# Twelve projection weights split during the first feed-forward stage, and the down weights of the passes loaded in pairs

## The chip, the cores and the metric

The kernel runs on one core of a Trainium2 chip. The metric is the device time of one execution in microseconds; the kernel before took 1989.62 us (median of three runs, 1989.21 to 1990.04). In what follows PE is the matmul engine, PEld its weight load, DVE the vector engine, ACT the scalar engine, POOL the GpSimd engine and SP the engine whose queue issues every DMA of this kernel.

## The reference, cut to what matters

One decoder layer on 1024 tokens with 16 meta tokens ahead of them, width 1024, all in float32:

```python
h = h + 0.5 * swiglu(rmsnorm(h, norm_ffn1), w_ffn1_gate, w_ffn1_up, w_ffn1_down)   # width 2816
u = rmsnorm(h, norm_mix)
qa, ka, va, qi, ki, wi, qs, ksw, vsw, ga, gb = split(u @ w_in)
# rope on qa, ka, qi, ki, qs, ksw
# sparse branch: scores from relu(qi . ki) * wi, the 256 largest keys, softmax attention with qa, ka, va
# window branch: 128 wide window with sinks, attention with qs, ksw, vsw
merged = sigmoid(ga) * (o_sparse @ w_branch_sparse) + sigmoid(gb) * (o_swa @ w_branch_swa)
h = h + merged @ w_out
h = h + 0.5 * swiglu(rmsnorm(h, norm_ffn2), w_ffn2_gate, w_ffn2_up, w_ffn2_down)
out = rmsnorm(h[:, BLOCK:], norm_final)
```

## The kernel before, in words

**Halves.** A float32 matrix is multiplied as two float16 halves, high and low. A weight tile of 128 rows arrives by DMA in a float32 buffer `wst` (two buffers). ACT writes its scaled high half into a float16 tile `wsp` (four buffers), and DVE writes the low half, which is the scaled weight less the high half (`split_w`, lines 428 to 431). PE then makes three products for each pair: high by high, high by low, low by high (`mm3`). A `wsp` buffer is free again when the last product that reads it is done.

**Stages.** The program is the first feed-forward network, the mixer (projections, rope, scores, the two attentions, the merge, the output projection) and the second feed-forward network. The tokens stand in two halves x = 0 and x = 1, of 528 and 512 columns.

**The feed-forward main part** multiplies 2 by 2 block matrices by seven products of quarter blocks (p1, p3 or p6, p7, p5, c11, p74, p53) and not eight, so each weight pair needs sums of its blocks first. One such round is a *joint* (lines 743 to 749); there are 32 of them, jobs 0 to 31, over gate, up and down weights. In joint i, `prepare(i + 1)` gives the steps that make job i + 1's weights: four sums or differences on DVE (tiles `sa`, `sb`), four high halves on ACT and four low halves on DVE (`wsp` for job halves x1 and x2, tiles x3 and x4 for the rest). The steps are put in a list `todo`, from which `pump` issues a share after each product; what is left is issued by `drain` at the joint's end. `fetch(i + 2)` issues the DMAs. The instructions issued this way have line 189 in the profile.

**The written order and the planner.** In the two stretches where `nc.on` is true, instructions are only recorded; `Plan.run` (lines 225 to 338) then orders them by a list schedule, taking on each engine the ready instruction of the lowest rank. The rank is the place in the program plus `nc.shift`. Instructions of a planned stretch have line 334. The planned stretches are: the beginning of the first network up to and with joint 0; everything from the end of the first network's main part to the end of the mixer; the beginning of the second network up to and with its joint 0; and the end. Joint 0 needs, besides `u` (the normalized input), the block sums `tb` of that input, which are made in the same stretch.

**The passes.** The last four of 22 blocks of the down projection, in each network, aren't done by joints but by a plain loop over x and over eight output blocks d: `load_w` loads a 128x512 weight, splits it, and PE multiplies (`pdn`), DVE adds to `h`.

**Projections in the mixer.** `k_half` and `q_groups` (lines 1187 to 1198) load two 128x1024 columns blocks of `w_in` each time (`load_w(win[...], 1024)`), for twenty loads in all: blocks 0 to 7 once for x = 0 and once for x = 1, blocks 8 to 11 once for both. They are used by `rope_split`, whose products are named `rp` in the profile.

```python
def load_w(src, n, st=None):
    ...
    sp = wsp_tile()
    nc.shift = -300
    split_w(sp, st, n)
    nc.shift = 0
    return sp
```

Of the kernel before, what the change touches and what calls it, by code (L numbers as in the profile page):

```python
# [11 lines left out]
F16 = mybir.dt.float16  # L12
F32 = mybir.dt.float32
I32 = mybir.dt.int32
U16 = mybir.dt.uint16
AF = mybir.ActivationFunctionType
ALU = mybir.AluOpType

P = 128
# [6 lines left out]
NF = DFF // P  # L26
# [10 lines left out]
WS = 256.0  # L37
# [316 lines left out]
def layer_kernel(ctx: ExitStack, tc: tile.TileContext, xT, gains, wgu1, wd1, win, wvi, wbs, wbw, wout,  # L354
# [78 lines left out]
    def wsp_tile():  # L433
        return new(big, [P, 2, 1024], F16, tag="wsp", name="wsp", bufs=4)

    def load_w(src, n, st=None):
        if st is None:
            st = load_raw(src, n)
# [5 lines that stand above are left out]
# [86 lines left out]
    def ffn(u, rb, hs, gi, wgu, wd, other_half, passes, saved, before_passes):  # L530
# [140 lines left out]
            split_w(x4, r2[:, hi], 512)  # L671
            return parts_of(x1, x2, x3, x4, 512)

        weights, fetched = {}, {}

        def fetch(i):
            if i < len(jobs):
                n = 2 * jobs[i][3]
                fetched[i] = [load_raw(src, n) for src in jobs[i][1:3]]

        def prepare(i):
            if i >= len(jobs):
                return []
            n = jobs[i][3]
            lo, hi, both = slice(0, n), slice(n, 2 * n), 2 * n
            r1, r2 = fetched.pop(i)
            x1, x2 = wsp_tile(), wsp_tile()
            sa, sb = sum_tiles()
            x3, x4 = late_tiles()
            weights[i] = parts_of(x1, x2, x3, x4, n)  # L690
            one, two = n / 750, n / 420
            v = nc.vector
            return [
                (0, lambda: high(x1, r1, both)),
                (one, lambda: v.tensor_add(sb[:, lo], r2[:, lo], r2[:, hi])),
                (0, lambda: high(x4, r2[:, hi], n)),
                (one, lambda: v.tensor_sub(sa[:, lo], sb[:, lo], r1[:, lo])),
                (one, lambda: v.tensor_sub(sa[:, hi], r1[:, lo], r2[:, lo])),
                (0, lambda: high(x2, sa, both)),
                (one, lambda: v.tensor_sub(sb[:, hi], r1[:, hi], sa[:, lo])),  # L700
                (two, lambda: low(x1, r1, both)),
                (one, lambda: low(x4, r2[:, hi], n)),
                (0, lambda: fetch(i + 1)),
                (0, lambda: high(x3, sb, both)),
                (two, lambda: low(x2, sa, both)),
                (two, lambda: low(x3, sb, both)),
            ]
# [32 lines left out]
        DOWN = ("p1", "p7", "p5", "p6", "c11", "p74", "p53")  # L740
        turn = [0]

        def joint(blocks, order):
            i = turn[0]
            turn[0] += 1
            own = prepare(i + 1)
            todo.extend(own[:7] + tail[:4] + own[7:10] + tail[4:] + own[10:])
            tail.clear()
            return fast(weights.pop(i), blocks, order)

# [304 lines left out]
        for x, subs, done in passes:  # L1055
# [1 line left out]
            full = c1 - c0 == hs[x][0].shape[1]  # L1057
            acc = new_acc()
            for d in range(KD):
                nd = (f1 - f0) * P  # L1060
                w = load_w(wd[d // 2][:, 2 * f0 * P + d % 2 * nd:2 * f0 * P + (d % 2 + 1) * nd], nd)
                if ph["mix"]:
                    for a, b in subs:
                        ps = mmps("pdn")[:, :b - a]
# [120 lines left out]
    wn = mcst([P, NB, 4], F32, "wn")  # L1185

    def k_half(x):
        w1, w2 = load_w(win[0], 1024), load_w(win[1], 1024)
        stack_k(rope_split(w1, w2, x, SUB_ALL[x]), kt[x], HW[x])

    def q_groups(xs, first, n):
        res = [[] for _ in xs]
        for g in range(n):
            w1 = load_w(win[first + 2 * g], 1024)
            w2 = load_w(win[first + 2 * g + 1], 1024)
            for lst, x in zip(res, xs):
                lst.append(q_half(w1, w2, x))
        return res
# [520 lines left out]
```

## Time and profile before

| what | us |
|---|---|
| median of three runs | 1989.62 |
| the profiled execution | 1987.38 |
| its span, first to last instruction | 1985.3 |
| PE busy in the span | 1918.0 |
| DVE busy | 1610.0 |
| ACT busy | 903.9 |
| POOL busy | 342.5 |

[...] The first network's main part runs from some 92 to 614 us, its passes to some 655, the mixer to 1340, the second network's main part to 1924. A busy PE is not always a PE at its peak: ends of matmuls are modelled and overlap the next one, so a short gap between two of them doesn't show as idle time. The page's chain of waits is 72% PE, 17% DVE, 6% ACT, 3% issue and 1% DMA.

### The profile page before, as it was taken

How to read it: one execution, taken by the hardware profiler on the slowest of the kernel's cores; microseconds unless marked ns; L12 is line 12 of the kernel's file. 1: busy time of each engine (PE TensorE's matmuls, PEld its weight loads, DVE VectorE, ACT ScalarE, POOL GpSimd, SP SyncE). 2: the span in 40 equal slices, each digit the busy share in tenths (PEclk: the TensorE clock that was granted, in tenths of full speed). 3: DMA queues.
4: the chain of work that ended last, by engine and by line, in shares of the span. 5: the costliest groups of instructions: out<-in, count | busy, mean ns of one | idle time of the engine just before them, and what ended most of it. 6: DMA issues, size and time to landing. Idle time of an engine off the chain costs nothing.

```text
span 1985.3 us, 32868 instructions
## 1 busy us (share of the span) xinstructions
PE 1918.0 (97%) x13080; PEld 1196.8 (60%) x13080; DVE 1610.0 (81%) x2809; ACT 903.9 (46%) x1621; POOL 342.5 (17%) x282
## 2 busy tenths in 40 slices
PE   6999999999998999899999999999899999999997
PEld 5688888888887656555545656444344444444443
DVE  7988788778775899999998967657987888788757
ACT  6533233233332546579876555435433333243232
POOL 0113311312210222221000000003312212312200
PEclk9999999999999999999999999999999999999998
DMA  5011211111222544221111231331112112111214
GB/s 173 22 60 49 65 64 49 59 65 38 70 75 87 185 150 132 69 91 44 45 37 49 92 112 38 128 122 39 47 53 66 53 58 58 54 64 50 78 33 138
DMA packets 60026, 146.96 MB, mean 74 GB/s; under 512 B 7392, under 2 KB 15584, under 8 KB 59872
## 3 DMA queue, kind: packets, MB, share of 16 engines
q1 hardware_dynamic: 59872, 144.87, 23.1%
q8 instruction: 102, 1.67, 0.4%
q14 instruction: 52, 0.43, 0.1%
HBM read 130.01 MB, written 14.76 MB: 73 GB/s over the span
## 4 chain that ended last, share of the span: by engine, by line
PE 72%; DVE 17%; ACT 6%; issue 3%; DMA 1%; SPq 0%; POOL 0%; DVEq 0%; ACTq 0%; POOLq 0%
PE pa L189 15%; PE pc L189 15%; PE pd L189 15%; PE pb L189 7%; PE p_gate L334 4%; PE p_out L334 4%; PE pdn L334 3%; DVE sc L334 3%; PE p_br L334 2%; DVE wsp L334 2%; ACT jk L334 2%; ACT psw L334 1%; DVE m L334 1%; PE rp L334 1%; DVE tb L334 1%
## 5 line engine op out<-in xcount | busy, mean ns | idle before, releaser
L189 PEld LDWEIGHTS <-wsp 128*128 128x128 f16 x4032 | 395.5, 98 | 205.7 <-DVE wsp L334 8.5
L334 PEld LDWEIGHTS <-wsp 128*128 128x128 f16 x3216 | 311.2, 99 | 295.9 <-issue 14.9
L189 PEld LDWEIGHTS <-x 128*128 128x128 f16 x3024 | 295.9, 98 | 145.1 <-issue 1.5
L189 PE MATMUL pa<-u,wsp 128*128 128x264 f16 (+1 forms) x1368 | 216.8, 313 | 7.8 <-DVE wsp L334 7.8
L334 PE MATMUL p_gate<-u,wsp 128*128 128x512 f16 x768 | 186.4, 379 | 0.0
L189 POOL TENSOR_TENSOR h<-h,base 128x512 f32<-128x512 f32 (+1 forms) x72 | 116.3, 1615 | 291.2 <-DVE base L189 210.5
L334 DVE SCALAR_TENSOR_TENSOR wsp<-wst,wsp 128x1024 f16<-128x1024 f32 (+2 forms) x131 | 133.1, 1019 | 38.7 <-ACT wsp L334 38.2
L334 ACT ACTIVATE wsp<-wst 128x1024 f16<-128x1024 f32 (+2 forms) x131 | 112.2, 861 | 92.3 <-PE p_out L334 28.5
L334 PE MATMUL rp<-u,wsp 128*128 128x512 f16 (+2 forms) x624 | 139.5, 365 | 3.9 <-DVE rt L334 3.5
L189 PE MATMUL pb<-tb,wsp 128*128 128x264 f16 (+1 forms) x684 | 106.8, 310 | 0.0
L189 PE MATMUL pc<-tb,x 128*128 128x264 f16 (+1 forms) x684 | 106.7, 310 | 0.1
L334 ACT ACTIVATE jk<-sc,s5nb 128x784 f16<-128x784 f32 (+2 forms) x93 | 98.0, 1054 | 16.1 <-DVE s5nb L334 14.7
L189 ACT ACTIVATE wsp<-wst 128x1024 f16<-128x1024 f32 (+1 forms) x60 | 57.9, 965 | 103.9 <-DMA wst<-in_wgu_dram 58.6
L189 PE MATMUL pd<-u,x 128*128 128x256 f16 (+1 forms) x684 | 105.2, 308 | 0.0
L189 PE MATMUL pc<-tb,wsp 128*128 128x256 f16 (+1 forms) x684 | 105.2, 308 | 0.0
L189 PE MATMUL pd<-tb,x 128*128 128x256 f16 (+1 forms) x684 | 105.2, 308 | 0.0
L189 PE MATMUL pa<-hid,wsp 128*128 128x264 f16 (+1 forms) x648 | 103.1, 310 | 0.0
L189 PE MATMUL pd<-hid,x 128*128 128x256 f16 (+1 forms) x648 | 101.6, 308 | 0.0
L189 ACT ACTIVATE wsp<-sa 128x1024 f16<-128x1024 f32 (+1 forms) x60 | 58.1, 968 | 95.3 <-DVE sa L189 95.3
L189 ACT ACTIVATE hid<-g 128x512 f16<-128x512 f32 (+1 forms) x54 | 33.2, 625 | 149.2 <-DVE g L189 149.2
L189 ACT ACTIVATE base<-pa 128x528 f32<-128x528 f32 (+1 forms) x62 | 37.1, 599 | 132.2 <-PE pa L189 132.2
L189 DVE TENSOR_TENSOR c<-pc,base 128x512 f32<-128x512 f32 x76 | 52.6, 692 | 55.1 <-PE pc L189 54.8
(238 smaller groups left out, 3478.0 us busy)
## 6 DMA issues: line engine op xcount, KB each, us to landing
wst<-in_wgu_dram SPq DMA_DIRECT2D x88, 512.0 KB, 4.0
wst<-in_win_dram SPq DMA_DIRECT2D x44, 512.0 KB, 3.5
wst<-in_wd_dram SPq DMA_DIRECT2D x48, 384.0 KB, 3.5
wst<-in_wd_dram SPq DMA_DIRECT2D x32, 256.0 KB, 2.9
wst<-in_wout_dram SPq DMA_DIRECT2D x16, 512.0 KB, 3.6
qscr<-ry SPq DMA_DIRECT2D x20, 256.0 KB, 2.2
q<-qscr SPq DMA_DIRECT2D x20, 256.0 KB, 3.0
wst<-in_wbs_dram SPq DMA_DIRECT2D x16, 256.0 KB, 3.3
```

The costliest lines, as they stand in the source:

```text
L189: return getattr(engine.real, op)(*[give(a) for a in args], **{k: give(v) for k, v in kw.items()})
L334: getattr(engine.real, op)(*[give(a) for a in args], **{k: give(v) for k, v in kw.items()})
```

## The change

Three edits are made.

1. *Ready weights.* In the first network's joints 1 to 25, one more group of steps, a *chore*, stands at the end of `todo`. A chore splits half a 128x1024 block of `w_in` (512 columns) into its float16 halves and stores them in device memory (`wready`); it also fetches the next half block. Twenty-four chores make the first twelve blocks. In the mixer, `load_ready` then loads the finished halves from device memory straight into a `wsp` tile, where `load_w` loaded float32 and split it. The buffers of the chores (`raw`, `pre`) come from the two buffers of tag `acc`.
2. *Pairs.* The passes load the down weights of two output blocks as one 128x1024 tile; two of the eight pairs of each network are fetched and split in joint 31, that is before the passes.
3. *Rank.* In `joint`, the weight steps of the next job are ranked by 300 places earlier (`ranked`). That has an effect only where the planner is on, so in joint 0 of each network.

```diff
+    ready = {}
+
+    def load_ready(m):
+        sp = wsp_tile()
+        nc.sync.dma_start(sp, ready[m])
+        return sp
+
+    def chores():
+        def fetch(c):
+            raw = new(big, [P, 528], F32, tag="acc", name="raw", bufs=2)
+            return raw, (0, lambda: nc.sync.dma_start(raw[:, :512], win[c // 2][:, c % 2 * 512:c % 2 * 512 + 512]))
+
+        def split(c, raw):
+            sp = new(big, [P, 2, 528], F16, tag="acc", name="pre", bufs=2)
+            if c % 2 == 0:
+                ready[c // 2] = new(dram, [P, 2, 1024], F16, name=f"wready{c // 2}")
+            dst = ready[c // 2][:, :, c % 2 * 512:c % 2 * 512 + 512]
+            return [(0, lambda: nc.scalar.activation(sp[:, 0, :512], raw[:, :512], AF.Copy, scale=WS)),
+                    (0.7, lambda: nc.vector.scalar_tensor_tensor(sp[:, 1, :512], raw[:, :512], WS, sp[:, 0, :512],
+                                                                 op0=ALU.mult, op1=ALU.subtract)),
+                    (0, lambda: nc.sync.dma_start(dst, sp[:, :, :512]))]
...
         def fetch(i):
-            if i < len(jobs):
+            if i == len(jobs):
+                fetched[i] = [load_raw(pair_src(d), 2 * ND) for d in range(2)]
+            elif i < len(jobs):
...
         def prepare(i):
-            if i >= len(jobs):
-                return []
+            if i == len(jobs):
+                ready_w.extend(wsp_tile() for _ in range(2))
+                return [(0, lambda op=op, x=x, r=r: op(x, r, 2 * ND)) for x, r in zip(ready_w, fetched.pop(i))
+                        for op in (high, low)]
...
+        def ranked(step):
+            def go():
+                was, nc.shift = nc.shift, -300
+                step()
+                nc.shift = was
+            return go
+
         def joint(blocks, order):
             i = turn[0]
             turn[0] += 1
-            own = prepare(i + 1)
+            own = [(c, ranked(step)) for c, step in prepare(i + 1)]
             todo.extend(own[:7] + tail[:4] + own[7:10] + tail[4:] + own[10:])
+            if gi == 0 and not nc.on and i % 1 == 0:
+                todo.extend(next(chore, []))
...
             for d in range(KD):
-                nd = (f1 - f0) * P
-                w = load_w(wd[d // 2][:, 2 * f0 * P + d % 2 * nd:2 * f0 * P + (d % 2 + 1) * nd], nd)
+                if d % 2 == 0:
+                    pair = ready_w.pop(0) if ready_w else load_w(pair_src(d // 2), 2 * ND)
+                w = pair[:, :, d % 2 * ND:(d % 2 + 1) * ND]
...
     def k_half(x):
-        w1, w2 = load_w(win[0], 1024), load_w(win[1], 1024)
+        w1, w2 = load_ready(0), load_ready(1)
...
-            w1 = load_w(win[first + 2 * g], 1024)
-            w2 = load_w(win[first + 2 * g + 1], 1024)
+            w1, w2 = load_ready(first + 2 * g), load_ready(first + 2 * g + 1)
```

The planner's order changes at several places; three of them matter later. On DVE, in the first network's joint 0 (planned), `wsp`, `sa`, `sb` and `x` are job 1's weight steps, `tb` and `tu` the block sums of the input and `hid` the hidden activations of the first blocks, which are needed only later. Before, the last rows of this stretch were:

```order
L334 TENSOR_TENSOR hid<-silu,hid 128x512
L334 SCALAR_TENSOR_TENSOR wsp<-wst,wsp 128x1024
L334 SCALAR_TENSOR_TENSOR x_592<-wst,x_592 128x512
L334 TENSOR_TENSOR hid<-silu,hid 128x528 x2
L334 SCALAR_TENSOR_TENSOR wsp<-sa,wsp 128x1024
L334 SCALAR_TENSOR_TENSOR x_992<-sb,x_992 128x1024
L189 TENSOR_TENSOR sb<-wst 128x512
```

Now the same steps stand between the second and the third group of `tb`, and the stretch ends with `hid` (`silu` here belongs to the first pair of blocks, `x_817` is job 1's x3):

```order
L334 SCALAR_TENSOR_TENSOR wsp<-wst,wsp 128x1024
L334 TENSOR_TENSOR sa<-sb,wst 128x512
L334 SCALAR_TENSOR_TENSOR silu<-pw,silu 128x512
L334 TENSOR_TENSOR sa<-wst 128x512
L334 TENSOR_TENSOR sb<-wst,sa 128x512
L334 SCALAR_TENSOR_TENSOR silu<-pw,silu 128x512
L334 SCALAR_TENSOR_TENSOR wsp<-sa,wsp 128x1024
L334 SCALAR_TENSOR_TENSOR x_817<-sb,x_817 128x1024
L334 TENSOR_TENSOR tu<-tu 128x512
```

So job 1's low halves moved from behind the last `tb` to a place ahead of two of the four `tb` groups. In the second network's joint 0 the move is of the same kind.

On SP's queue, at the beginning of the mixer, `wst<-in_win` were the float32 loads of projection weights, `hspill` stores of the residual, `kscr` and `k` the key's way through device memory. Before:

```order
L334 DMA wst<-in_win_dram 128x1024
L334 DMA hspill<-h 128x512 x2
L334 DMA wst<-in_win_dram 128x1024
L334 DMA hspill<-h 128x512
L334 DMA wst<-in_win_dram 128x1024
L334 DMA wst<-in_wvi_dram 128x980
L334 DMA wst<-in_wvi_dram 128x588
L334 DMA wst<-in_win_dram 128x1024
L334 DMA kscr<-ry 128x1056
```

Now (the numbers in `wready_...` tell the blocks apart):

```order
L334 DMA wsp<-wready_1684 128x2048
L334 DMA hspill<-h 128x512 x2
L334 DMA wsp<-wready_2087 128x2048
L334 DMA hspill<-h 128x512 x2
L334 DMA wsp<-wready_2426 128x2048
L334 DMA hspill<-h 128x512
L334 DMA wst<-in_wvi_dram 128x980
L334 DMA kscr<-ry 128x1056
```

The loads stand at about the same places of the queue, but they now write a `wsp` tile, and so wait for one to be free, where before they waited for a `wst` buffer.

## Rows read from the trace of the kernel before

**Rows 1.** Stretches: us, PE, PEld, DVE, ACT, POOL busy, clock, DMA, GB/s

```profile
...
92.00:614.00 522.00, 522.00 (x4694) 459.50 (x4692) 402.84 (x509) 172.52 (x251) 110.22 (x68) 1.00 0.19 59
614.00:655.00 41.00, 34.98 (x256) 25.51 (x254) 27.17 (x59) 16.50 (x31) 0.95 (x1) 0.96 0.48 150
655.00:905.00 250.00, 234.58 (x1766) 142.36 (x1765) 237.47 (x577) 153.23 (x367) 67.88 (x56) 0.99 0.38 122
905.00:1075.00 170.00, 168.81 (x1166) 89.76 (x1164) 159.41 (x475) 145.47 (x317) 7.62 (x37) 1.00 0.12 38
1075.00:1340.00 265.00, 264.03 (x1846) 144.60 (x1843) 192.32 (x373) 128.06 (x211) 6.04 (x24) 1.00 0.30 95
1340.00:1420.00 80.00, 70.38 (x313) 31.66 (x313) 68.66 (x85) 39.41 (x59) 33.72 (x20) 0.96 0.12 40
...
```

**Rows 2.** Chain of waits: start, us, what

```profile
1241.55 5.18 PE p_gate L334 x24
```

**Rows 3.** Timeline, joint 0 and job 1 of the first network

```profile
77.41 1.92 DVE L334 TENSOR_TENSOR tb<-tu,tb 128x512 f16<-128x512 f32 x3
...
86.60 0.61 PE L189 MATMUL pa<-u,wsp 128*128 128x264 f16 x4
...
90.96 3.83 PE L189 MATMUL pa<-u,wsp 128*128 128x264 f16 x20 [3.75 <-DVE wsp L334]
```

**Rows 4.** Timeline, joint 0 and job 1 of the second network

```profile
1387.37 2.29 DVE L334 SCALAR_TENSOR_TENSOR wsp<-sa,wsp 128x1024 f16<-128x1024 f32 x1
...
1406.42 0.67 DVE L334 TENSOR_TENSOR tb<-tu,tb 128x512 f16<-128x512 f32 x1
...
1409.68 0.59 PE L189 MATMUL pa<-u,wsp 128*128 128x512 f16 x2
...
1414.29 3.96 PE L189 MATMUL pa<-u,wsp 128*128 128x512 f16 x10 [4.01 <-DVE wsp L334]
...
1415.96 1.21 DVE L334 SCALAR_TENSOR_TENSOR wsp<-sa,wsp 128x1024 f16<-128x1024 f32 x1
```

**Rows 5.** Waits of PE, whole span: us in total, times, longest

```profile
...
PE pa L189 <- DVE wsp L334: 7.8, 2, 4.0
...
PE pdn L334 <- DVE wsp L334: 3.3, 1, 3.3
...
PE pdn L334 <- ACT wsp L334: 1.7, 1, 1.7
...
```

**Rows 6.** Timeline, first passes

```profile
616.56 1.30 DVE L189 TENSOR_TENSOR hid<-c,hid 128x528 f16<-128x528 f32 x2
...
619.27 6.79 PE L334 MATMUL pdn<-hid,wsp 128*128 128x272 f16 x44 [3.32 <-DVE wsp L334]
...
627.78 19.49 PE L334 MATMUL pdn<-hid,wsp 128*128 128x272 f16 x157 [1.71 <-ACT wsp L334]
```

**Rows 7.** Groups on DVE, then ACT, 614 to 905 us: busy, mean ns

```profile
L334 DVE SCALAR_TENSOR_TENSOR wsp<-wst,wsp 128x1024 f16<-128x1024 f32 x22 | 30.1, 1367 | 4.4 <-ACT wsp L334 4.4
...
L334 DVE SCALAR_TENSOR_TENSOR wsp<-wst,wsp 128x512 f16<-128x512 f32 x18 | 12.4, 699 | 1.5 <-ACT wsp L334 1.5
...
L334 ACT ACTIVATE wsp<-wst 128x1024 f16<-128x1024 f32 x22 | 23.0, 1049 | 14.4 <-PE rp L334 7.5 <-DMA wst<-in_win_dram 6.1 <-PE pv_t L334 0.7
```

**Rows 8.** Chain of waits, 655 to 905 us, shares by line

```profile
by line: DVE sc L334 11.8%; ACT psw L334 10.9%; PE rp L334 10.1%; issue 8.8%; DVE wsp L334 6.7%; DVE psw L334 5.7%; DVE rt L334 4.0%; DMA wst<-in_win_dram 3.8%; PE pv_t L334 3.7%; ACT wsp L334 3.7%; DVE pts L334 2.9%; DVE m L334 2.8%; ACT j
```

**Rows 9.** Stretch 655 to 905 us, tile wsp alone: PE, PEld, DVE, ACT busy

```profile
655.00:905.00 250.00, 182.15 (x937) 68.91 (x720) 37.69 (x31) 29.05 (x31) 0.99 0.38 122
```

**Rows 10.** DMA issues: KB each, us from issue to landing

```profile
wst<-in_win_dram SPq DMA_DIRECT2D x44, 512.0 KB, 3.5
```

**Rows 11.** Waits, 655 to 905 us: total, times, longest

```profile
ACT wsp L334 <- PE rp L334: 15.7, 7, 3.9
```

**Rows 12.** Group of 512-wide low halves in the joints: busy, mean ns

```profile
L189 DVE SCALAR_TENSOR_TENSOR x<-wst,x 128x512 f16<-128x512 f32 x36 | 24.5, 681 | 0.0
```

**Rows 13.** Timeline, end of a joint in the first network

```profile
110.79 0.69 DVE L189 TENSOR_TENSOR base<-pd,base 128x512 f32<-128x512 f32 x1 [1.17 <-PE pd L189]
```

More of the change, by code (lines that the diff above doesn't have):

```diff
@@ L434, in wsp_tile @@
         return new(big, [P, 2, 1024], F16, tag="wsp", name="wsp", bufs=4)
+    ready = {}
[16 more added lines that the diff above has]
+                    (0, lambda: nc.sync.dma_start(dst, sp[:, :, :512]))]
+        raw, step = fetch(0)
+        yield [step]
+        for c in range(24):
+            done = split(c, raw)
+            if c < 23:
+                raw, step = fetch(c + 1)
+                done.append(step)
+            yield done
+    chore = chores()
     def load_w(src, n, st=None):
@@ L672, in wide_weights, with pair_src @@
             return parts_of(x1, x2, x3, x4, 512)
-        weights, fetched = {}, {}
+        weights, fetched, ready_w = {}, {}, []
+        F0 = F_GROUPS[-1][0]
+        ND = (NF - F0) * P
+        def pair_src(j):
+            return wd[j][:, 2 * F0 * P:2 * F0 * P + 2 * ND]
         def fetch(i):
-            if i < len(jobs):
+            if i == len(jobs):
+                fetched[i] = [load_raw(pair_src(d), 2 * ND) for d in range(2)]
+            elif i < len(jobs):
                 n = 2 * jobs[i][3]
```

## The prediction

> **What bounds the kernel now.** I read the table by stretches first, then PE's waits, then the chain of waits in the one stretch where PE is not full, and last the timelines at the four places where the change moves something. In the first network's main part PE is busy for all of 522.00 us while DVE works 402.84 and ACT 172.52: PE bounds it, and DVE has 119 us to spare [rows 1]. In the passes PE is busy 34.98 of 41 us. In the mixer from 655 to 905 us PE is busy 234.58 of 250 and DVE 237.47 of 250, 95%: DVE is the fuller of the two. From 905 to 1340 PE is again above 99%, and DVE falls to 73% in the last 265 us. At the second network's start both have holes (70.38 and 68.66 of 80). So time can come back only where PE has holes: before 92 us, 614 to 905, 1340 to 1420 and in the tail. The idle time that the rows show from 614 to 905 is 6.0 + 15.4 = 21.4 us, and there is more that they hide: 24 matmuls of 512 columns take 5.18 us, so 216 ns each [rows 2], and every gap below a matmul's modelled end counts as busy.
>
> **The first joint of the first network (rank).** Before, PE came to job 1 at 86.60 us, did 4 matmuls and stood 3.75 us for a low half (`wsp`); the other 20 began at 90.96 [rows 3]. Taking 112 ns for one of the 4, PE started as if at 90.5. Now job 1's steps stand ahead of the last `tb` groups. From 77.41 us, 1.92 us for three, the last `tb` began at about 78.65 before [rows 3]. By the order, DVE now has ahead of it, in addition: three 1024-wide low halves (1.21 us each in [rows 4], some 1.15 from start to start), one 512-wide, four sums, one `hid` and two `c` (0.6 each), which is 8.25 us. The last `tb` then begins at 86.9 and the one before it ends at 86.4; PE still has 4 matmuls of p6 and the 24 of p74 to do, 0.45 + 2.7 us, and reaches job 1 at 89.6 with its weights ready. Gain 90.5 - 89.6 = 0.9 us. Bounds: -1 (another us of `tb`) and 3.8 (the whole stall).
>
> **The same in the second network.** PE reached job 1 at 1409.68, did 2, stood 4.01 us and went on at 1414.29, as if started at 1413.86 [rows 4]. The last `tb` began at 1406.42. Newly ahead of it: three 1024-wide low halves, one 512-wide and three sums, 5.8 us; gone from ahead: two `silu` and two `hid`, 2.4. So it begins 3.4 us later, at 1409.8, and the one before it ends near 1408.4; then 2 matmuls of p6 and 12 of p74 at 216 ns, 3.0 us: job 1 at 1411.2 or so. Gain 2.7 us. POOL is the risk here: next to its work the same low half took 2.29 us where it took 1.21 later [rows 4], and two such moved into that stretch leave 0.6. Bounds 0 and 4. [...]
>
> **The passes (pairs).** PE stood 3.32 us until 619.27 for the first low half and 1.71 us until 627.78 for a high half [rows 5, 6]. With two pairs split before, both go. What is late next is the low half of the last `hid`: DVE has it from 616.56, 1.30 us for two, so PE's first group is held until about 617.2, and ends about 2.5 us earlier than it did. With the second stall this is 4 us (bounds 0 and 5). In joint 31 the four new splits lie beside a PE that is full; DVE needs 2.4 us for them, in a part where it has 119 us to spare. In the second network's passes PE shows no wait for weights, so I count nothing there.
>
> **The mixer (ready weights).** Removed are 20 splits of 1024 columns. In 614 to 905 us a low half costs DVE 1.367 us and a high half ACT 1.049 [rows 7]: 27.3 us of DVE and 21.0 of ACT. The pairs remove a little more DVE time there (16 of 0.699 give way to 6 of 1.367, 3.0 us). How much of that is on the path? On the chain from 655 to 905 the low halves hold 6.7% of 250 us, 16.8 us, the high halves 3.7% and the float32 loads 3.8%, 18.8 us together [rows 8]. All low halves of that stretch hold DVE 37.69 us [rows 9]; the twenty removed, at 27.3, are 73% of that, and 73% of 16.8 is 12.2. I take 12 us. The upper bound is all DVE time, 27: DVE is at 95%, and if nothing else held it every microsecond taken from it would come off the stretch. The lower bound is below nothing: a load of the same 512 KB took 3.5 us to land [rows 10], and it now has to start after a `wsp` tile is free, where before only the two splits (1.05 + 1.37 = 2.4 us) came after that; seven times the split waited for PE to release such a tile, 15.7 us in all [rows 11]. If 20 loads each end 1.1 us later than the splits did, 22 us are lost. What covers it: four tiles hold two weight pairs, and one weight keeps PE for 5.18 us [rows 2], so a freed tile has some 10 us before its turn. I cost it at nothing. After 905 PE is full, and the work that it has to do is the same, so the 12 us stay.
>
> **The chores.** Each adds a high half on ACT, which is busy a third of that part [rows 1], one low half of 0.681 us on DVE [rows 12] and two DMAs, behind all other steps of a joint. Its place is ahead of the last sum of the joint, for which DVE waits 1.17 us on PE [rows 13]: 0.68 fits into 1.17. DVE's idle time in the main part, 119 us over 31 joints, is 3.8 us for each. On SP, the store waits for that low half, and the next `wst` fetch is queued behind it; that fetch comes half a joint later. I cost 24 chores at nothing. Without that cover they cost 24 x 0.68 = 16.3 us.
>
> **Sum.** 0.9 + 4 + 12 + 2.7 = 19.6 us. The profiled execution took 1987.38 us (span 1985.3 and 2.1 around it), so 1967.8; the median of the runs stands 2.2 us above that execution, so I predict 1970.
>
> **Rivals.**
> (a) DVE's time isn't what holds the mixer: attention's chain of `psw`, `sc` and issue on ACT, DVE and PE, over 30% of [rows 8], takes the place of the splits. For it: `ACT psw` and `issue` have 19.7% of the chain. Against it: DVE at 95%. Then only the other terms count: 1989.6 - 7.6 = 1982.
> (b) More of the chain goes than the low halves: 73% of the 18.8 us of high halves and loads goes too, 13.7 us: 1956. For it: DVE has no holes to fill otherwise. Against it: the new load is on the chain at the same place.
> (c) The chores push PE: DVE's low half meets a product that has to be drained, or POOL's adds, and each costs its whole 0.68 us: 1970 + 16.3 = 1986, no change or nearly. For it: PE has no hole there at all, so any loss counts. Against it: 1.17 us of waiting at the very place.
> (d) The slower side: the `wsp` tiles. If the ready weights wait for a tile that PE frees less than 3.5 us before it needs the next one, DMA landing takes the place of the splits, and SP's in-order queue holds the q and k stores behind it. Price: the 12 us are not gained, and 20 x 1.1 are lost: 1989.6 - 7.6 + 22 = 2004. It decides from the point where the tile is free less than 3.5 us ahead of its use. For it: [rows 11]. Against it: the 10 us above.
>
> **How the numbers follow.** Two per mille, 4 us, is what a measurement of this kernel can tell from no change. Chances: forecast (1960 to 1977) 0.56; (a) 0.18; (b) 0.11; (c) 0.08; (d) 0.07. Range: 1957 takes in most of (b), 1985 all of (a); (d), most of (c) and a part of (b) stay outside, 0.2. Forecast, (a) and (b) are faster, 0.85, less a point for errors of (a)'s small sum: 0.84. Same is (c), 0.08. Slower is (d) and that point, 0.08.
>
> **What would show it.** In the changed kernel's profile: no PE wait at job 1 in either network and p74 ending some 3 us later than before; PE's `pdn` without its two stalls; no `wsp<-wst` of `w_in` blocks 0 to 11 between 655 and 905, and the first `p_gate` some 16 us nearer to the first `pdn`, with PE's idle time between 614 and 905 nearer 8 than 21. The main part of the first network must still take 522 us less the shift of its start; if it takes more, (c) is right. PE or PEld waiting for a DMA into `wsp` would show (d). The forecast is wrong if DVE stays at 95% there and PE's holes stay too.

## The result and the profile after

The changed kernel took 1975.58 us (median of four runs, 1974.48 to 1977.38), the kernel before on the same chip 1989.83 us (1989.21 to 1991.28). The ratio is 0.9932 with a 95% interval of 0.9920 to 0.9944: 13.5 us faster, 11 to 16. Forecast were 1970 us and a gain of 19.6.

The two profiled executions lie closer together: 1976.26 us (span 1974.5) against 1987.38, 11.1 us. Before's happened to be 2.5 us under the median of its runs, after's 0.7 us over; that is the rest of the 14 us. Between the same landmarks of the two traces (start times of the first matmul of a group) the time went like this:

| stretch | before, us | after, us | difference | forecast |
|---|---|---|---|---|
| start to product p6 of job 1, first network | 94.63 | 96.63 | +2.0 | -0.9 |
| main part, to the first `pdn` | 520.72 | 521.02 | +0.3 | 0 |
| passes, to the first `rp` | 52.29 | 49.32 | -3.0 | -4 |
| mixer, first `rp` to the first `pg` of the second network | 672.94 | 663.44 | -9.5 | -12 |
| second network, first `pg` to p6 of job 1 | 77.47 | 73.58 | -3.9 | -2.7 |
| main part, to the first `pdn` | 506.05 | 507.71 | +1.7 | 0 |
| passes, first to last `pdn` | 44.25 | 47.00 | +2.7 | 0 |
| last `pdn` to the end | 16.91 | 15.75 | -1.2 | 0 |

Two of these differences are partly chance. Of the first one, 0.9 us arise before any edit: 48 `pw` matmuls after 18.8 us took 7.38 us before and 8.23 after, and in the runs below, whose code is the same there, between 7.08 and 8.31. So the loss that belongs to the rank there is 1.1 us. The last one too varies without an edit: in the run with the chores alone the tail took 15.2 us.

The stretches of the changed kernel, which answer to [rows 1] (us, then busy time of PE, PEld, DVE, ACT, POOL, the granted clock as a share of its upper level, DMA share, GB/s; the mean clock of the execution was 0.992 before and is 0.993 after):

```profile
92.00:614.00 522.00, 522.00 (x4697) 459.46 (x4696) 419.92 (x537) 187.51 (x278) 111.44 (x69) 1.00 0.27 81
614.00:655.00 41.00, 37.52 (x280) 28.22 (x278) 30.05 (x57) 16.39 (x25) 0.95 (x1) 0.96 0.57 175
655.00:905.00 250.00, 241.47 (x1821) 147.01 (x1819) 228.92 (x607) 141.02 (x367) 63.92 (x59) 0.99 0.36 116
...
1420.00:1924.00 504.00, 501.06 (x2311) 226.26 (x2310) 395.75 (x505) 173.85 (x254) 109.26 (x68) 1.00 0.19 57
```

In the first row DVE took on 17.1 us of chores and PE is still full. In the third DVE fell from 237.47 to 228.92 us although work of later stages has moved up into the stretch, and PE rose by 6.9. The last row isn't full any more; before, PE was busy for 503.90 us of it.

PE's waits, against [rows 5] (total, times, longest):

```profile
PE pd L334 <- ACT tb L334: 4.6, 2, 4.2
...
PE pdn L334 <- DVE wsp L189: 3.7, 2, 2.2
PE pb L334 <- ACT tb L334: 3.0, 1, 3.0
...
PE pc L189 <- DVE c L189: 1.6, 2, 1.0
```

The waits for `wsp` at job 1 are gone, as are those of `pdn` for the planned splits. In their place stand longer waits for `tb` in ACT's queue, and two kinds that were not there: for `wsp` of line 189 (the pairs of joint 31), and for `c` in the second network's joints 1 and 2. Of the waits for `tb`, the one of 3.0 us is new and lies in the first network's joint 0. The one of 4.2 us lies in the second network's joint 0 (4.24 us at 1392.56), where before one of 3.05 us stood. The first network's and the two new kinds are followed up below.

**The start of the first network.** PE at the end of joint 0, which answers to [rows 3]:

```profile
88.42 0.38 PE L334 MATMUL pb<-tb,wsp 128*128 128x264 f16 x2 [2.96 <-ACT tb L334]
88.65 0.86 PE L334 MATMUL pc<-tb,wsp 128*128 128x256 f16 x4
89.30 1.09 PE L334 MATMUL pb<-tb,wsp 128*128 128x264 f16 x4
90.29 3.80 PE L334 MATMUL pc<-tb,x 128*128 128x264 f16 x24
93.93 2.86 PE L189 MATMUL pa<-u,wsp 128*128 128x264 f16 x24
```

ACT there:

```profile
87.20 0.64 ACT L334 ACTIVATE hid<-silu 128x528 f16<-128x528 f32 x1 [2.93 <-POOL silu L334]
87.75 1.16 ACT L334 ACTIVATE tb<-tu 128x528 f16<-128x528 f32 x2
```

DVE, behind that `tb`, and POOL, ahead of that `hid`:

```profile
88.40 0.71 DVE L334 TENSOR_TENSOR tb<-tu,tb 128x528 f16<-128x528 f32 x1 [1.77 <-ACT tb L334]
```

```profile
83.15 4.02 POOL L334 TENSOR_TENSOR silu<-silu,t 128x512 f32<-128x512 f32 x1 [6.71 <-ACT tb L334]
```

PE waits for a `tb`, ACT has it behind a `hid` in its queue, and that `hid` waits for POOL's sum, which took 4.02 us. The same sum took 1.28 us before. Meanwhile DVE did `tu` and `tb` at 0.68 us each, their usual time. So in this meeting of the two engines POOL's instruction took 2.74 us longer and DVE's no longer.

The granted clock of those moments, as stretches of the same view as above:

```profile
84.00:88.00 4.00, 0.97 (x6) 0.57 (x6) 2.63 (x5) 1.07 (x3) 3.16 (x1) 1.00 0.00 0
88.00:90.00 2.00, 1.58 (x10) 1.18 (x10) 1.16 (x2) 0.91 (x2) 0.00 (x0) 0.71 0.00 0
90.00:94.00 4.00, 4.00 (x27) 2.99 (x26) 3.88 (x7) 1.23 (x2) 0.00 (x0) 0.72 0.01 4
94.00:98.00 4.00, 4.00 (x38) 3.47 (x37) 3.87 (x6) 3.13 (x5) 1.31 (x1) 1.00 0.00 0
```

After the waits, the last of 2.96 us, the granted clock fell from 1.00 to a mean of 0.71 and then 0.72, and the 24 matmuls at 90.29 took 3.80 us where 24 of that form took 2.86 before (at 83.90, clock 1.00).

**The pairs.** DVE at the end of the first network's joint 31, and PE at the start of the passes, against [rows 6]:

```profile
616.91 0.69 DVE L189 TENSOR_TENSOR base<-pd,base 128x512 f32<-128x512 f32 x1 [1.17 <-PE pd L189]
617.63 0.69 DVE L189 SCALAR_TENSOR_TENSOR g<-base,g 128x512 f32<-128x512 f32 x1
618.24 2.35 DVE L189 SCALAR_TENSOR_TENSOR wsp<-wst,wsp 128x1024 f16<-128x1024 f32 x2
620.51 0.70 DVE L189 TENSOR_TENSOR hid<-g,hid 128x528 f16<-128x528 f32 x1
```

```profile
619.52 0.75 PE L334 MATMUL pdn<-hid,wsp 128*128 128x272 f16 x5 [1.47 <-DVE wsp L189]
621.27 10.51 PE L334 MATMUL pdn<-hid,wsp 128*128 128x272 f16 x77 [1.00 <-DVE hid L189]
```

The two low halves stand behind the joint's last sum and ahead of the last `hid`, just before PE needs them. In this joint DVE had little else to do. In the second network the same order makes PE wait 2.22 us at 1914.52, where before it waited 0.60.

**The second network's joints 1 and 2.** PE waits for `c` to be drained from `pc`:

```profile
1415.50 2.75 PE L189 MATMUL pc<-tb,x 128*128 128x512 f16 x12 [0.99 <-DVE c L189]
1434.43 2.75 PE L189 MATMUL pc<-tb,x 128*128 128x512 f16 x12 [0.64 <-DVE c L189]
```

The first pair's `hid` now comes after the `tb`, so DVE began job 2's sums at 1410.50, 9.1 us after job 1's first matmul (1401.40) and 6.5 us after p6 of job 1 had begun (1403.99). Before, DVE began them 1.0 us after p6 (1419.08 after 1418.05). In the six traces that rank all steps in the second network, its main part took 507.7 us; in the six without the rank, 506.0 to 506.9.

### The profile page after: what moved, and what is told of

Read it like the earlier page. It is cut to its first block, busy times and chain, and to the rows that moved or that the text cites. A ratio compares the mean times of both kernels' runs of the same rounds, so it can differ in the third digit from the quotient of the medians.

```text
span 1974.5 us, 32864 instructions
## 1 busy us (share of the span) xinstructions
PE 1916.1 (97%) x13080; PEld 1197.8 (61%) x13080; DVE 1603.1 (81%) x2797; ACT 896.1 (45%) x1609; POOL 341.9 (17%) x282
## 4 chain that ended last, share of the span: by engine, by line
PE 78%; DVE 12%; ACT 6%; issue 3%; POOL 1%; DMA 0%; SPq 0%; DVEq 0%; ACTq 0%; POOLq 0%
PE pc L189 15%; PE pa L189 14%; PE pd L189 14%; PE pb L189 7%; PE p_gate L334 6%; PE pdn L334 4%; PE p_out L334 4%; PE p_br L334 3%; PE rp L334 3%; DVE sc L334 2%; ACT jk L334 2%; PE ptr L334 1%; PE pw L334 1%; ACT psw L334 1%; PE pv_b L334 1%
## 5 line engine op out<-in xcount | busy, mean ns | idle before, releaser
L334 DVE SCALAR_TENSOR_TENSOR wsp<-wst,wsp 128x512 f16<-128x512 f32 (+2 forms) x91 | 98.9, 1089 | 32.7 <-ACT wsp L334 32.3
L334 ACT ACTIVATE wsp<-wst 128x512 f16<-128x512 f32 (+2 forms) x91 | 84.1, 929 | 64.2 <-PE p_out L334 31.1
L334 PE MATMUL p_br<-oT,wsp 128*128 128x512 f16 x384 | 94.9, 379 | 0.0
```

What stands on the lines that cost most here:

```text
L334: getattr(engine.real, op)(*[give(a) for a in args], **{k: give(v) for k, v in kw.items()})
```

## The experiments

All were timed against the kernel before on the same chip. A gain in us that goes with a ratio is (1 - ratio) x 1989. Where two changed kernels are compared with each other, they may have run on different chips; the kernel before had medians of 1988.77 to 1989.83 on these.

### The three edits one at a time

These three are the kernel before with one edit of the change each. Ready weights, with `chores` and `load_ready` as in the change:

```diff
+            if gi == 0 and not nc.on and i % 1 == 0:
+                todo.extend(next(chore, []))
...
-        w1, w2 = load_w(win[0], 1024), load_w(win[1], 1024)
+        w1, w2 = load_ready(0), load_ready(1)
...
-            w1 = load_w(win[first + 2 * g], 1024)
-            w2 = load_w(win[first + 2 * g + 1], 1024)
+            w1, w2 = load_ready(first + 2 * g), load_ready(first + 2 * g + 1)
```

> The kernel before with the chores and the ready weights alone. Theory (DVE's time holds the mixer from its first projections to p_gate, chores are free): the trace of the changed kernel has that stretch 8.5 us shorter with all three edits in; so 8 to 10 us faster than before, about 1981, and the first joints' main part unchanged. Rival (some of those 8.5 us come from the pairs, which take 3 us of DVE time out of the same stretch): 5 to 6 us, 1984. Rival (the chores cost something that the other two edits hid): under 5 us.

Measured: 1978.43 us, ratio 0.9944 (0.9931 to 0.9956), 11.1 us faster, somewhat more than the 8 to 10 expected. From the first `rp` to the first `pg` the trace took 662.8 us against 672.9 before: 10.1. So the ready weights alone are near the 12 us of the forecast, and the pairs took nothing out of the mixer: with them alone that stretch took 672.9, as before.

Pairs alone:

```diff
+            if i == len(jobs):
+                fetched[i] = [load_raw(pair_src(d), 2 * ND) for d in range(2)]
...
+                if d % 2 == 0:
+                    pair = ready_w.pop(0) if ready_w else load_w(pair_src(d // 2), 2 * ND)
+                w = pair[:, :, d % 2 * ND:(d % 2 + 1) * ND]
```

> The kernel before with the pairs alone. My step: 4 us faster, all in the first network's passes, 1986. Theory after the trace of the changed kernel: 3 us gained there, 2 us lost at the start of the second network's passes (PE waits 2.2 us for a low half that DVE writes only at the end of joint 31), and 1 us gained at the tail: 1987 to 1989.

Measured: 1985.88, ratio 0.9984 (0.9975 to 0.9993), 3.2 us faster, nearer to the step of the forecast than to the 1987 to 1989 read off the trace of the changed kernel. The trace shows 4.4 us won in the first network's passes and 2.8 lost in the second's. The 4.4, where the changed kernel has 3.0, comes from the matmuls behind the same two waits of 1.47 and 1.00 us: the 77 that took 10.51 us there, with a granted clock of 0.66 from 620 to 624 us and 0.91 from 624 to 628, took 9.11 here:

```profile
619.74 9.11 PE L334 MATMUL pdn<-hid,wsp 128*128 128x272 f16 x77 [1.00 <-DVE hid L189]
```

Rank alone:

```diff
-            own = prepare(i + 1)
+            own = [(c, ranked(step)) for c, step in prepare(i + 1)]
```

> The kernel before with the rank alone, in both networks. My step: 0.9 + 2.7 = 3.6 us faster, 1986. Theory after the trace of the changed kernel: the first network loses 1 us (block sums tb on ACT wait behind a hid half that waits for POOL), the second gains 3.9 in joint 0 and gives 1.6 back in joints 1 and 2: 1 us faster or so, 1988 to 1989.5.

Measured: 1987.45, ratio 0.9991 (0.9982 to 0.9999), 1.8 us faster; half of what the step had. By its trace the first network's joint 0 loses 1.0 us, the second network's wins 4.0, and the second main part gives 1.7 back.

The three gains add to 16.1 us; together they measured 13.5 (11 to 16), so a loss between them can't be told from chance.

### What of the mixer's gain is DVE's

Both kernels start from the one with the ready weights alone. In the first only the low half comes from device memory, and ACT still makes the high one; in the second it is the other way round.

```diff
     def load_ready(m):
+        st = load_raw(win[m], 1024)
         sp = wsp_tile()
-        nc.sync.dma_start(sp, ready[m])
+        nc.sync.dma_start(sp[:, 1, :], ready[m][:, 1, :])
+        nc.scalar.activation(sp[:, 0, :], st[:, :1024], AF.Copy, scale=WS)
         return sp
```

```diff
-        nc.sync.dma_start(sp, ready[m])
+        nc.sync.dma_start(sp[:, 0, :], ready[m][:, 0, :])
+        nc.vector.scalar_tensor_tensor(sp[:, 1, :], st[:, :1024], WS, sp[:, 0, :],
+                                       op0=ALU.mult, op1=ALU.subtract)
```

> As the run with ready weights alone, but each of the twenty loads brings only the low half from device memory; the float32 tile is still loaded and ACT still writes the high half from it. DVE loses its 20 low halves, ACT and the float32 loads keep everything. Theory (DVE's time): most of the gain of the ready weights stays, 6 to 9 us faster than before, 1981 to 1984. Rival (the high halves and the float32 loads on the chain are as much of it): half of it, 4 to 5 us, 1985.

> The mirror: each of the twenty loads brings only the high half from device memory; the float32 tile is still loaded and DVE still writes the low half from both. ACT loses its 20 high halves, 21 us of busy time; DVE keeps everything. Theory (DVE's time): 0 to 2 us faster than before, 1988 to 1990. Rival (high halves matter as much as low ones): 4 to 5 us, 1985.

Measured: low half ready 1978.76, ratio 0.9948 (0.9935 to 0.9960), 10.3 us; high half ready 1985.20, ratio 0.9978 (0.9969 to 0.9987), 4.4 us. The stretch from 655 to 905 us of the two, low first, then high:

```profile
655.00:905.00 250.00, 238.45 (x1816) 146.10 (x1814) 231.21 (x612) 161.40 (x392) 63.97 (x61) 1.00 0.45 144
```

```profile
655.00:905.00 250.00, 235.13 (x1776) 142.57 (x1774) 235.97 (x572) 135.37 (x349) 68.47 (x56) 1.00 0.44 143
```

Taking 27 us of low halves from DVE gives nearly all of the 11.1, more than the 6 to 9 expected, with ACT busier than before (161.40 against 153.23). So the time was DVE's. But taking the high halves alone from ACT also gave 4.4, which is what the rival had and not the 0 to 2 of the theory, though DVE is nearly as full as before. Each low half waits for its high half, so an earlier high half can let DVE do it earlier: of the 4.4 us that DVE waited for high halves of this size [rows 7] none are left in this trace, and 2.6 us of waits for DMAs stand there instead. That this is all of the gain is argued, not shown. By the traces the two together give more than both at once (9.1 + 3.2 against 10.1 us from the first `rp` to the first `pg`), so in part they are two ways to the same time; the times alone (10.3 + 4.4 against 11.1, each with an interval of some 2 us to either side) can't tell.

### The price of the chores

The chores run, but the mixer still loads float32 and splits it.

```diff
-        w1, w2 = load_ready(0), load_ready(1)
+        w1, w2 = load_w(win[0], 1024), load_w(win[1], 1024)
```

> The kernel before with the 24 chores in the first network's joints, while the mixer still loads float32 and splits it; what the chores stored isn't read. Prices the chores alone. Theory (they lie in DVE's and ACT's idle time): 1989 to 1991, within 1 us of before. Rival (each low half on DVE pushes PE by its whole 0.68 us): 16 us slower, 2006.

Measured: 1988.04, ratio 0.9992 (0.9983 to 1.0001): nothing. Its main part:

```profile
92.00:614.00 522.00, 522.00 (x4688) 459.06 (x4686) 418.47 (x533) 184.49 (x274) 110.15 (x68) 1.00 0.27 82
```

### The pairs, issued earlier in joint 31

`pump` issues steps until their costs use up a share of the joint's total cost. In joint 31 all steps at the start cost 0, so the share is 0, and nothing is issued until `drain`, at the joint's end.

```diff
-                return [(0, lambda op=op, x=x, r=r: op(x, r, 2 * ND)) for x, r in zip(ready_w, fetched.pop(i))
-                        for op in (high, low)]
+                return [(c, lambda op=op, x=x, r=r: op(x, r, 2 * ND)) for x, r in zip(ready_w, fetched.pop(i))
+                        for c, op in ((0, high), (1.2, low))]
```

> The changed kernel, with a cost of 1.2 for each low half of the two pairs in the list of joint 31, where it is 0; so they are issued after that joint's first two products and not at its end. Theory (the pairs' low halves stand in DVE's queue behind the joint's last product and ahead of the last hid, and this is all that PE waits for at the start of both passes): 2 to 2.5 us in each network, 4 to 5 us faster than the changed kernel, 1971, and no wait of pdn for wsp. Rival (the last hid is late by itself, the low halves only hide it): under 1 us, 1975.

Measured: 1969.69 (1969.16 to 1970.21), ratio 0.9901 (0.9886 to 0.9916), 5.9 us under the changed kernel's median. DVE in the second network's joint 31, then PE:

```profile
1893.42 1.22 DVE L189 SCALAR_TENSOR_TENSOR wsp<-wst,wsp 128x1024 f16<-128x1024 f32 x1 [1.70 <-ACT wsp L189]
1895.25 1.23 DVE L189 SCALAR_TENSOR_TENSOR wsp<-wst,wsp 128x1024 f16<-128x1024 f32 x1 [0.61 <-ACT wsp L189]
```

```profile
1911.23 18.94 PE L334 MATMUL pdn<-hid,wsp 128*128 128x512 f16 x87 [0.60 <-DVE hid L189]
```

The low halves are done over 12 us before the first `pdn` (1908.96), in time in which DVE waited. No `pdn` waits for `wsp` any more; the first passes took 45.65 us (49.32 in the changed kernel, 52.29 before), the second 43.68 (47.00, 44.25).

### The rank

Rank in the second network only, on the changed kernel:

```diff
-            own = [(c, ranked(step)) for c, step in prepare(i + 1)]
+            own = prepare(i + 1)
+            if gi:
+                own = [(c, ranked(step)) for c, step in own]
```

> The changed kernel, with the rank in the second network's joint 0 only. Theory (the rank loses in the first network what the trace shows at its joint 0, 1.1 us beside a 0.9 us difference in the first 48 matmuls that the rank can't make): 1 us faster than the changed kernel, 1974.5. Rival (the rank is worth its 0.9 us there, as my step had it): 1 us slower, 1976.5.

Measured: 1974.69 (1974.46 to 1975.92), ratio 0.9928 (0.9916 to 0.9941). The runs overlap with the changed kernel's, so by itself this decides nothing.

The same beside the early pairs, so both edits:

```diff
+                        for c, op in ((0, high), (1.2, low))]
...
+            if gi:
+                own = [(c, ranked(step)) for c, step in own]
```

> The changed kernel with two of its edits mended: the pairs' low halves issued early in joint 31, and the rank in the second network alone. Theory (the two add up: 5.9 us by the run with early pairs, 0.9 by the run with the rank in the second network): 1968.8. Rival (they share something): 1969.7 or more.

Measured: 1967.34 (1966.26 to 1968.38), ratio 0.9892 (0.9877 to 0.9907), 2.3 us under the kernel with the early pairs, whose runs lie all above, and more than the theory had. The rank does lose in the first network; how much of the 2.3 is chance is said at the end of this section.

Then the planner's idea of POOL, on the kernel with the early pairs; it is set back after the first planned stretch:

```diff
-            t = 0.2 + n * 0.0023 if op.startswith("tensor_t") or op in ("tensor_sub", "tensor_add", "tensor_mul") \
+            t = 0.2 + n * Plan.pool_k if op.startswith("tensor_t") or op in ("tensor_sub", "tensor_add", "tensor_mul") \
...
+    pool_k = 0.0075
...
+                            Plan.pool_k = 0.0023
```

> As the kernel with the early pairs, rank in both networks; the planner takes POOL's sums in the first planned stretch for 0.2 + 0.0075 us per column instead of 0.2 + 0.0023, so 4.0 us for 512 columns, which is what one of them took beside DVE. By the order, PE's instructions stay as they are; on ACT the high half of hid that waits for POOL now stands behind the last tb high halves. Theory (in the first network's joint 0 PE waits 2.96 us for tb because ACT's queue stands at that hid): the wait goes, the first network's job 1 starts about 2 us earlier, 1967.7. Rival (the last tb groups are late on DVE anyway): another wait of the same size takes its place, 1969.7.

Measured: 1968.80 (1967.08 to 1969.27), 0.9 us under the early pairs where 2 were expected, and the runs of the two overlap: inconclusive. The trace has PE waits of 0.93, 0.84, 0.24 and 1.40 us for `tb` where one of 2.96 was the largest, so most of the wait did come back, as the rival had it. The clock fell all the same:

```profile
88.78 4.74 PE L334 MATMUL pc<-tb,x 128*128 128x264 f16 x24
```

```profile
86.00:90.00 4.00, 3.05 (x14) 1.97 (x14) 4.00 (x8) 0.64 (x1) 0.83 (x2) 0.50 0.02 4
```

Fewer steps ranked: only those for x1 and x2 (in both networks), with POOL's cost as above.

```diff
-            own = [(c, ranked(step)) for c, step in prepare(i + 1)]
+            own = [(c, step if k in (2, 6, 8, 10, 12) else ranked(step)) for k, (c, step) in enumerate(prepare(i + 1))]
```

> As the run with POOL's cost, and only the steps that make job 1's x1 and x2 are ranked; the steps for x3 and x4, which joint 1 reads later, are not (in both networks). Theory (the fewer low halves stand ahead of the last tb groups, the earlier these end): in each joint 0 about 2 us of DVE less ahead of them, 1 to 2 us faster than the run with POOL's cost. Rival (x3 and x4 are then late in joint 1, and PE waits for them there): same or slower.

Measured: 1962.85 (1962.53 to 1963.61), ratio 0.9871 (0.9854 to 0.9887). That is 6.0 us under the kernel with POOL's cost alone, three times the most that was expected. By the traces the first network's joint 0 gives 4.2 us of it (25.6 to 21.3, see the end of this section). The second network's joint 0, where a gain was expected too, gives 0.2, and its main part 1.1. A part of the 6.0 is the chance told of there. PE at the end of the first network's joint 0:

```profile
84.09 0.60 PE L334 MATMUL pc<-tb,wsp 128*128 128x256 f16 x4 [1.41 <-DVE tb L334]
...
85.93 2.86 PE L334 MATMUL pc<-tb,x 128*128 128x264 f16 x24 [0.61 <-DVE c L334]
88.63 2.86 PE L189 MATMUL pa<-u,wsp 128*128 128x264 f16 x24
```

And the clock over it:

```profile
82.00:86.00 4.00, 1.96 (x15) 1.29 (x14) 3.63 (x7) 1.29 (x2) 1.49 (x1) 1.00 0.00 0
86.00:90.00 4.00, 4.00 (x37) 3.47 (x37) 4.00 (x7) 1.65 (x3) 1.31 (x1) 1.00 0.02 4
```

The waits are shorter, and the clock stays at its upper level after them: the 24 matmuls take 2.86 us and not 4.74 as in the run with POOL's cost.

The last kernel has the same ranks, with POOL's cost set back:

```diff
-    pool_k = 0.0075
+    pool_k = 0.0023
```

> As the run with x1 and x2 alone ranked, with POOL's cost in the planner back at 0.0023: on ACT the high half of hid that waits for POOL stands ahead of the last two tb high halves again. Theory (in the first network this hid holds the last tb on ACT): 1 to 2 us slower than that run, 1964 to 1965, and PE waits for ACT's tb again in the first network's joint 0. Rival (the order of these two on ACT is worth nothing, as the difference of 0.9 us between the runs with early pairs without and with POOL's cost may be noise): 1962.9. Against the changed kernel it tells what all of x3's and x4's steps ahead of tb cost.

Measured: 1964.82 (1964.30 to 1965.96), ratio 0.9876 (0.9860 to 0.9893), 2.0 us above the kernel just told of, and no execution of the one is as fast as the slowest of the other. ACT, PE and the clock in it:

```profile
83.30 0.64 ACT L334 ACTIVATE hid<-silu 128x528 f16<-128x528 f32 x1 [2.92 <-POOL silu L334]
```

```profile
84.53 0.39 PE L334 MATMUL pb<-tb,wsp 128*128 128x264 f16 x2 [2.47 <-ACT tb L334]
...
86.13 4.53 PE L334 MATMUL pc<-tb,x 128*128 128x264 f16 x24 [0.25 <-DVE c L334]
```

```profile
86.00:90.00 4.00, 3.87 (x20) 2.75 (x20) 3.73 (x7) 1.23 (x2) 0.11 (x1) 0.57 0.01 4
```

ACT's queue stands at the `hid` again, PE waits 2.47 us for the `tb` behind it, and the clock falls to 0.57. So with x3 and x4 out of the way the order of the two on ACT is worth 2 us. With all steps ranked it was worth 0.9 us that can't be told from nothing: there DVE's own low halves, ahead of the `tb`, hold PE nearly as long.

Chance plays a part ahead of joint 0 too. In two traces, those of the early pairs and of POOL's cost, 79 `pw` matmuls took 10.69 us, with the granted clock at 0.65 and 0.74 from 36 to 40 us, where they took 9.02 or 9.03 in all the others. The changed kernel, whose code up to there is that of the early pairs, is one of these others, so it is chance:

```profile
33.88 10.69 PE L334 MATMUL pw<-u,wsp 128*128 128x256 f16 x79 [0.41 <-DVE silu L334]
```

Free of that, the time from joint 0's first `pb` (its product p3) to p6 of job 1 puts all of these side by side. It is 24.8 us before, and 24.9 to 25.1 in the seven other traces without the rank in the first network. With the rank it is 25.9 in the changed kernel, 25.8 with the rank alone and 26.4 with the early pairs, so the rank loses 1 us or so there (1.4 of the 2.3 us between the early pairs with it and without it). It is 25.6 with POOL's cost, 24.0 with x1 and x2 ranked, and 21.3 with both.

## Why the prediction was right and where it was wrong

The direction, the place of the largest gain and its cause were right, and the time lies in the range. The gain was 13.5 us and not 19.6. Two steps failed (1 and 2), one term was somewhat too large (3), one came near by luck (4), and a cost is missing from three terms of the sum (5).

1. **The passes: the step "In the second network's passes PE shows no wait for weights, so I count nothing there" failed**, and with it "with two pairs split before, both go". I took the new splits to lie early in joint 31, beside a full PE. They are written into the list with cost 0, so they are issued at the joint's end, and DVE has them between the last sum and the last `hid`. That cost 2.7 us in the second network, which had no stall to lose, and kept the first at 3.0 of 4 us (4.4 in the run with the pairs alone). With the splits early the first passes are 6.6 us shorter than before, the second 0.6: 5.9 us of time, the largest miss. DVE's order at the joint's end would have told it.
2. **The first network's rank: the step "The last `tb` then begins at 86.9 ... reaches job 1 at 89.6" failed.** DVE itself was about where the step had it: it was done with what stood ahead at 86.6, but then stood 1.77 us for ACT, and the last two `tb` began at 88.40 and 90.16. The step took DVE for the only queue. A `tb` needs ACT first, where it stood behind a `hid` that waits for POOL. PE did job 1 without a stall, but came to it at 93.93, or 93.0 without the 0.9 us of chance, 3.4 later than forecast. The wait that had gone at job 1 came back inside joint 0. Instead of a gain of 0.9 the loss is 1.1 (25.9 against 24.8).

   Where the 3.4 us come from, by an estimate from the rows above: the last `tb` came 1.1 us later than the step had it (88.42 less 0.9, against 86.4). PE then had 34 matmuls to do and not 28, which is 0.7. And these took 5.5 us where 34 take 3.8 at a clock of 1.00, which is 1.7.

   The run with POOL's cost shows that ACT wasn't all: there the last `tb` began on DVE at 86.7 (without what that trace lost ahead of joint 0, 0.7 us), as forecast. But PE, after four shorter waits, did its last 32 matmuls in 6.4 us, at a clock of 0.50 and 0.67, and came to job 1 at 92.7. So besides the queue it was the clock that the step had wrong.

   What a wait of one instruction did to those behind it stands in ACT's rows of the changed kernel: DVE began the last `tu` at 84.73 us and took 0.69 for it, and ACT began the two `tb` only at 87.75, behind the `hid` for which it had stood 2.93 us.
3. **The mixer's 12 us** were the right mechanism and slightly too much: 11.1 alone by time, 10.1 alone and 9.5 beside the other edits by the trace. The chain's share of the low halves (16.8 us), times 73%, was a fair estimate; all of DVE's 27 us would have been far off. What is late next are the projections' own products. The chain from 655 to 905 us, against [rows 8]:

```profile
by line: PE rp L334 23.0%; DVE sc L334 14.8%; ACT psw L334 8.7%; issue 6.8%; PE pdn L334 4.9%; DVE psw L334 4.3%; DVE rt L334 4.0%; ACT jk L334 3.5%; DVE m L334 3.2%; DVE pts L334 2.7%; PE pv_s L334 2.3%; ACT pts L334 1.8%; PE ptr L334 1.7%
```

   `wsp` and the loads have left it, and `rp` on PE has more than doubled, from 10.1%. PE's idle time from 614 to 905 us fell from 21.4 to 12.0, where I expected nearer 8, and the first `p_gate` came 11.5 us nearer to the first `pdn`, not 16.
4. **The second network's rank** won 3.9 us in joint 0 and gave 1.7 back in joints 1 and 2, through the late `hid`: 2.2, near the 2.7. That nearness is luck. The place of job 1 was right: the forecast 1411.2 (1411.4, if its own 1408.4 and 3.0 are added) came out as 1411.6 on the time scale of the kernel before (1401.40, counted from the first `pg`). The gain there was larger than 2.7 because removing the stall also removed the slow clock behind it (5; 0.60 from 1414 to 1418 us before, 1.00 from 1400 to 1408 in the changed kernel), and the 1.7 given back weren't in the sum. The feared meeting of DVE with POOL did not make the three moved low halves longer (1.21 us each); one of POOL's sums took 3.25 us beside them, where the longest in the same place before took 2.25. In the first network, where the step had 1.15 us for each, two of the three were longer (1.69 and 1.66).
5. **The clock after a stall is missing.** The sum priced each stall of PE at its length. But in the kernel before each of the three longest of them (3.75, 3.32 and 4.01 us) was followed by a stretch at a lower clock. These are the stretches around the matmuls that ended the stalls, at 90.96, 619.27 and 1414.29:

```profile
90.00:94.00 4.00, 3.04 (x15) 2.13 (x16) 4.00 (x6) 0.44 (x1) 0.00 (x0) 0.57 0.49 156
```

```profile
620.00:624.00 4.00, 4.00 (x24) 2.97 (x23) 0.87 (x2) 0.14 (x1) 0.00 (x0) 0.63 0.73 185
```

```profile
1414.00:1418.00 4.00, 3.71 (x10) 1.37 (x11) 4.00 (x6) 0.22 (x1) 0.00 (x0) 0.60 0.67 228
```

   There 20 matmuls took 3.83 us [rows 3] where 24 take 2.86, 44 took 6.79 [rows 6] where 77 take 9.11, and 10 took 3.96 [rows 4] where 12 take 2.75. That is 1.4 to 1.6 us more for each, by an estimate from these numbers. So the stalls were worth some 4.6 us more than the sum had. It explains why the second network's joint 0 gave 3.9, and why the first passes gave 6.6 once the pairs were early, above the bound of 5.

The **chores** cost next to nothing, as forecast: the main part is 0.3 us longer in each trace with them, and alone they measured no change. 24 low halves took 17.3 us of DVE:

```profile
L189 DVE SCALAR_TENSOR_TENSOR pre<-raw,pre 128x512 f16<-128x512 f32 x24 | 17.3, 723 | 0.2
```

Of the rivals, (a) is out, since the ready weights alone gave 11.1 us where it had none; (b) is out, since its 25 us of mixer are more than twice what the ready weights alone gave; (c) is out by the run with the chores. (d) is out too: a ready weight took 4.4 us to land where a float32 one took 3.5 [rows 10],

```profile
wsp<-wready SPq DMA_DIRECT2D x20, 512.0 KB, 4.4
```

but no PE wait for it shows in the changed kernel.

The best version of these runs has all three edits with the two mended (early pairs; only x1 and x2 ranked, and POOL's sums planned at their price beside DVE): 1962.85 us, 25.7 us under the kernel before and 12.7 under the changed one.

## What to carry to other kernels

Work that is to be done "earlier" is only earlier where it is issued: look up its place in the order of each engine, at the start and at the end of the stretch, before counting a stall as gone. When a step is moved ahead of another, follow every engine that the delayed one passes through, not only the one on which the move was made; and move only what is needed first. Price a stall of PE with what the granted clock did behind it, and not at its length alone. Here the share of the chain of waits was a good estimate of what a removed instruction is worth on an engine that is 95% busy, where its busy time was more than twice too much.

## What the runs showed of the hardware

- Behind some waits of PE the granted clock was lower, and the matmuls there took longer. Near the end of the first network's joint 0 are 24 matmuls that took 2.86 us at a clock of 1.00. In the changed kernel, after a wait of 2.96 us, the clock was 0.71 and then 0.72, and they took 3.80; in the last kernel, after one of 2.47, it was 0.57 and they took 4.53. With the rank alone, after 2.96 us, they took 3.32; with the early pairs, after 2.97, 3.89.
- The length of the longest wait didn't tell whether that happened. In the run with POOL's cost, after waits of 0.93, 0.84, 0.24 and 1.40 us, the clock was 0.50 and the same 24 matmuls took 4.74 us; with x1 and x2 alone ranked on top of that, after two of 1.41 and 0.61 us, it stayed at 1.00 and they took 2.86. After the same two waits of 1.47 and 1.00 us, 77 matmuls took 10.51 us in the changed kernel and 9.11 in the one with the pairs alone.
- A sum on POOL of 512 columns, 1.28 us before, took 4.02 us beside `tu` and `tb` on DVE, while DVE's own took their usual 0.68. In other meetings it was DVE's that took longer. Before, the same sum kept its 1.28 us and two `hid` that DVE began after it took 2.06 us, where two took 1.31 ten us later; in the changed kernel a low half beside POOL took 1.69 us and not 1.22:

```profile
80.09 1.28 POOL L334 TENSOR_TENSOR silu<-silu,t 128x512 f32<-128x512 f32 x1 [8.04 <-DVE hid L334]
```

```profile
80.47 2.06 DVE L334 TENSOR_TENSOR hid<-silu,hid 128x528 f16<-128x528 f32 x2
```

```profile
73.61 1.69 DVE L334 SCALAR_TENSOR_TENSOR wsp<-sa,wsp 128x1024 f16<-128x1024 f32 x1
```
